# Two rows of weights side by side over the first chunk of x

## The chip, the cores and the metric

The kernel runs on one core of a Trainium2 chip. The metric is the device time in microseconds of one execution; a kernel's time is the median of its runs. The engines are named as in the profile: PE is TensorE (matmuls), PEld its weight loads, DVE is VectorE, ACT is ScalarE, POOL is GpSimd, SP is SyncE, which here only issues DMAs. ACT issues a few DMAs too.

## The reference

One inference step of a two-layer decoder trunk: a prompt of 1024 tokens and 8 x 4 sample tokens, 1056 tokens in all, of width 1024. Layer 0 is a gated linear recurrence with a short convolution, layer 1 a gated linear recurrence with a matrix state; a final norm follows. What matters here is how layer 0 starts:

```
xf = x.astype(jnp.float32)
xn = xf * lax.rsqrt(jnp.mean(xf * xf, axis=-1, keepdims=True) + EPS) * gain
u = xn @ w_in                       # (tokens, 1024) @ (1024, 3072)
xb, gate = u[..., :W_LRU], u[..., W_LRU:]
xc, new_buf = _causal_conv(xb, conv_w, conv_b, buf)
h, h_last = _rg_lru(xc, w_r, b_r, w_i, b_i, lam, h0)
y = h * silu(gate)
x = x + y @ w_out
```

## The kernel before

Everything lies transposed: features on the 128 partitions, tokens along the free dimension. The 1056 tokens are three chunks of 352 (`CH`, index `c`), the 1024 features of x eight blocks of 128 (index `k`). A row of weights is one 128-wide slice of the output features: 128 x 1024 numbers, which come in two halves of 512 columns; the first half serves blocks 0 to 3 of x, the second blocks 4 to 7.

Each fp32 operand is split into a rounded part and a remainder, hi and lo, and a product takes three matmuls (`mm3`, lines 241 to 245: hi by hi, lo by hi, hi by lo). For a half row of weights that means one DMA into `wraw` (or another free tile: `a`, `ST`), one cast on ACT into `whi` (L378) and one subtraction into `wlo` (L323). For a block of x of the first chunk it is one DMA into `sg`, one ACT instruction into `xh` (L861) and one DVE instruction into `xl` (L867). The step of a row over one block is the three matmuls, and eight steps fill one PSUM bank of the four called `mm` (mm_156 to mm_159, taken in turn).

The first chunk is not normalised before it is multiplied. Its squares are summed aside (`squares`: L428 on POOL or L430 on ACT, then the sums on DVE, L433, into `xb`), `norm` (L277, L445 to L453) makes the factor of each token, and the evacuation of a bank multiplies by it (L527 for a gate row, L480 for a convolution row). Chunk 1 is normalised first (L458, its sums of squares in `R`), then split again (L459, L323) and multiplied. Six rows come first, three gate rows and three convolution rows (`items = gate(0) + conv(0, True)`); `products(c)` goes through them chunk by chunk. Row 4 is the fifth, and takes the bank of row 0 again.

48 dummy matmuls (`WARM`, L728: ones by ones into a bank that nobody reads) keep PE busy until the first data are there. They wait for nothing and have the lowest priority.

The order on all five engines comes from a planner. The code of the layer first records operations in a `Flow` (engine, estimated us, what is read, what is written, a priority); `plan` lists them by priority as they become ready, `back` derives due times from the end, eight turns of that are tried, and `search` then changes keys at random in the first 60 us, 3000 times with a fixed seed, and keeps what brings a late PE instruction no later. What is recorded with `main=True` keeps its own order: each main PE operation depends on the one recorded before it, so the steps run in the order in which they are recorded. For these first products each step is an operation of its own (`product(..., 1, ...)`). The order found is written into the program as it stands, so each engine goes through its list in order and waits where something isn't there yet.

```
def product(w, xs, step=8, more=()):
    ps, pk = next(mm)
    ...
        fl.add("PE", 0.48 * len(ks), emit, (...), (pk,), 1, main=True)
    return ps, pk
```

## Time and profile before

| what | us |
|---|---|
| three runs | 1062.17, 1062.39, 1063.31; median 1062.39 |
| the profiled execution | 1062.88 |
| its span, first to last instruction | 1061.1 |
| PE busy in the span | 1051.4 |
| DVE busy | 843.7 |
| ACT busy | 588.2 |
| POOL busy | 542.0 |

The profile shows one execution. A line of instructions gives start and duration in us, engine, source line, operation, written tile and read tiles, shapes, and how many; in brackets the engine's idle time before it and what ended that. Matmuls are pipelined: one of 352 columns is shown with 0.32 us, but the next starts 0.16 us later, so a step takes 0.48. PE being busy therefore does not say that it does useful work: the dummies count too.

### The profile page before, as it was taken

What the parts mean: (1) busy time and instruction counts of PE and PEld (TensorE: products, weight loads), DVE (VectorE), ACT (ScalarE), POOL (GpSimd) and SP (SyncE); (2) the same over time, 40 slices, a digit from 0 to 9 for tenths busy, and PEclk for the clock granted to TensorE, in tenths of its full rate; (3) what the DMA queues carried; (4) which work ended last, traced back from release to release, by engine and by line L of the source; (5) the groups of instructions that cost most, each with busy time, mean ns of one, the idle gap of its engine ahead of it and who ended that gap; (6) DMA issues with size and microseconds to landing.
All of it is one profiled execution on the core that took longest, in us unless ns stands there. A gap on an engine that the chain in (4) does not pass through costs nothing.

```text
span 1061.1 us, 25695 instructions
## 1 busy us (share of the span) xinstructions
PE 1051.4 (99%) x9972; PEld 1025.8 (97%) x9972; DVE 843.7 (80%) x1677; ACT 588.2 (55%) x1329; POOL 542.0 (51%) x604
## 2 busy tenths in 40 slices
PE   9999999999999999999999999999999999999997
PEld 9999999999999999999999999999999999999996
DVE  7999996888888689265799988978879797994435
ACT  6568656867675875243354474646464645652323
POOL 3425443444444455555677656555555565642544
PEclk9999999999999999999999999999999999999997
DMA  9201112123742685440210131312121212354204
GB/s 301 64 26 45 54 51 74 57 61 108 240 150 61 182 287 165 133 130 28 73 51 30 44 101 45 101 37 89 44 83 53 85 58 74 113 181 156 85 1 164
DMA packets 70121, 103.07 MB, mean 97 GB/s; under 512 B 9200, under 2 KB 51184, under 8 KB 70000
## 3 DMA queue, kind: packets, MB, share of 16 engines
q1 hardware_dynamic: 67696, 98.67, 29.9%
q10 hardware_dynamic: 2304, 2.77, 0.8%
q8 instruction: 78, 1.28, 0.5%
q14 instruction: 43, 0.35, 0.1%
HBM read 71.05 MB, written 25.49 MB: 91 GB/s over the span
## 4 chain that ended last, share of the span: by engine, by line
PE 89%; DVE 7%; POOL 1%; DMA 1%; issue 1%; ACT 0%; POOLq 0%; ACTq 0%; DVEq 0%
PE mm L243 24%; PE mm L244 24%; PE mm L245 24%; PE hg L567 1%; PE hg L1052 1%; PE hg L1161 1%; PE hg L1271 1%; DVE R L1368 1%; PE hg L1217 1%; PE hg L243 1%; PE hg L244 1%; PE hg L245 1%; PE hg L1273 1%; DMA wraw<-in_w_dram 1%; DVE tmp L1368 1%
## 5 line engine op out<-in xcount | busy, mean ns | idle before, releaser
L243 PE MATMUL mm<-xh,whi 128*128 128x352 f32 (+1 forms) x1143 | 358.8, 314 | 0.0
L245 PE MATMUL mm<-xh,wlo 128*128 128x352 f32 (+1 forms) x1143 | 353.4, 309 | 0.0
L244 PE MATMUL mm<-xl,whi 128*128 128x352 f32 (+1 forms) x1143 | 353.4, 309 | 0.0
L323 POOL TENSOR_TENSOR wlo<-wraw,whi 128x256 fp32r<-128x256 f32 (+3 forms) x184 | 203.2, 1121 | 178.7 <-ACT whi L378 79.9
L244 PEld LDWEIGHTS mm<-xl,whi 128*128 128x128 f32 x1143 | 215.3, 188 | 1.5
L243 PEld LDWEIGHTS mm<-xh,whi 128*128 128x128 f32 x1143 | 215.0, 188 | 1.5
L245 PEld LDWEIGHTS mm<-xh,wlo 128*128 128x128 f32 x1143 | 215.0, 188 | 0.0
L499 DVE SCALAR_TENSOR_TENSOR k<-xb,prm_sb,k 128x352 f32<-128x352 f32 (+2 forms) x144 | 90.0, 636 | 10.9 <-ACT k L496 7.7
L243 PE MATMUL mm<-t,whi 128*128 128x264 f32 (+1 forms) x306 | 89.4, 292 | 0.0
L244 PE MATMUL mm<-t,whi 128*128 128x264 f32 (+1 forms) x306 | 87.8, 287 | 0.0
L245 PE MATMUL mm<-t,wlo 128*128 128x264 f32 (+1 forms) x306 | 87.6, 286 | 0.0
L1501 DVE TENSOR_TENSOR k<-mm,k 128x264 f32<-128x264 f32 x144 | 60.2, 426 | 20.6 <-PE mm L245 17.5
L323 POOL TENSOR_TENSOR wlo<-R,whi 128x256 fp32r<-128x256 f32 x64 | 60.0, 957 | 24.7 <-ACT whi L1428 24.7
L582 POOL TENSOR_TENSOR k<-X 128x352 f32<-128x352 f32 x36 | 43.9, 1228 | 47.8 <-DVE R L583 38.2
L378 ACT CAST whi<-wraw 128x512 fp32r<-128x512 f32 (+2 forms) x83 | 46.1, 574 | 30.0 <-PE mm L244 15.7
L243 PEld LDWEIGHTS mm<-t,whi 128*128 128x128 f32 x306 | 57.7, 188 | 0.2
L245 PEld LDWEIGHTS mm<-t,wlo 128*128 128x128 f32 x306 | 57.8, 189 | 0.0
L244 PEld LDWEIGHTS mm<-t,whi 128*128 128x128 f32 x306 | 57.7, 189 | 0.0
L1428 ACT CAST whi<-wraw 128x512 fp32r<-128x512 f32 x52 | 32.1, 619 | 36.3 <-PE mm L245 16.8
L243 PE MATMUL mm<-yh,whi 128*128 128x352 f32 x153 | 50.0, 327 | 0.0
L245 PE MATMUL mm<-yh,wlo 128*128 128x352 f32 x153 | 49.4, 323 | 0.0
L244 PE MATMUL mm<-yl,whi 128*128 128x352 f32 x153 | 49.4, 323 | 0.0
(479 smaller groups left out, 2640.9 us busy)
## 6 DMA issues: line engine op xcount, KB each, us to landing
wraw<-in_w_dram SPq DMA_DIRECT2D x90, 256.0 KB, 2.8
wraw<-in_wo_dram SPq DMA_DIRECT2D x34, 192.0 KB, 2.6
si<-in_s_in_dram SPq DMA_DIRECT2D x8, 512.0 KB, 3.6
out_ss_out_dram<-si SPq DMA_DIRECT2D x8, 512.0 KB, 2.6
R<-in_w_dram SPq DMA_DIRECT2D x15, 256.0 KB, 2.6
sg<-x1b SPq DMA_DIRECT2D x21, 176.0 KB, 3.0
x<-sg SPq DMA_DIRECT2D x21, 176.0 KB, 1.9
R<-td SPq DMA_DIRECT2D x72, 44.0 KB, 2.0
```

Of the source, the lines that this page charges most:

```text
L243: T.matmul(out, wh, xh, start=first, stop=False)
L244: T.matmul(out, wh, xl, start=False, stop=False)
L245: T.matmul(out, wl, xh, start=False, stop=last)
L323: emit = lambda: e.tensor_tensor(b, x, a.bitcast(F32), op=ALU.subtract)
L378: act(m, lambda hi=hi, raw=raw, m=m: S.copy(hi[:, :m], raw[:, :m]), rk, (hk,), prio)
L499: dve(u, lambda src=src, dst=dst, sh=sh, k=k: V.scalar_tensor_tensor(dst, sh(src, k), pc("cw", 12 * k + m), dst, op0=ALU.mult, op1=ALU.add ...
L567: fl.add("PE", 0.62, lambda ps=ps, i=i, c=c: T.matmul(ps[:96, :CH], gs[:, i, :], ST[:96, chunk(c)], start=True, stop=True), (("gs",), *((" ...
L582: pool(CH, lambda x=x, a=a, b=b: G.tensor_tensor(x, a.bitcast(F32), b.bitcast(F32), op=ALU.add), (ak, bk), (xk,), 3)
L1052: T.matmul(ps[32 * j:32 * j + 32, n * w:n * w + w], B[:, o:o + 32], q(slice(o, o + 32)), start=True, stop=True, tile_position=(0, 32 * j))
L1368: dve(n, lambda: V.tensor_tensor(o, a, b, op=op), r, (w,), prio, True)
L1428: act(512, lambda: S.copy(hi, raw), (rk,), (hk,), 2)
L1501: dve(QT, lambda: V.tensor_tensor(o[0], z[0], u[0], op=ALU.add), (z[1], u[1]), (o[1],), 0)
```

## The change

`side_by_side` takes the first two rows (`SIDE = 2`, both gate rows) over chunk 0. It takes a bank for each, and records the steps block by block: block 0 for row 0, block 0 for row 1, block 1 for row 0, and so on; then both banks are evacuated. The other four rows, and all rows over chunks 1 and 2, are recorded as before.

```diff
+SIDE = 2
...
+        def side_by_side(w, xs):
+
+            got = [next(mm) for _ in w]
+            n = len(xs)
+            for k in range(n):
+                for i, (ps, pk) in enumerate(got):
+                    fl.add("PE", 0.48, lambda k=k, i=i, ps=ps: mm3(ps[:, :CH], w[i](k)[:2], *xs[k][:2], k == 0, k == n - 1),
+                           (*xs[k][2], *w[i](k)[2]), (pk,), 1, main=True)
+            return got
+
         def products(c):
-            for i in (2, 0, 1, 3, 4, 5) if c else range(6):
+            if c == 0:
+                for i, got in enumerate(side_by_side(ws[:SIDE], xcols(0))):
+                    items[i][1](0, *got, bcs)
+            for i in (2, 0, 1, 3, 4, 5) if c else range(SIDE, 6):
                 items[i][1](c, *product(ws[i], xcols(c), 1, more=later[i]), *([] if c else [bcs]))
```

Since the planner lists the operations anew, more moves than the diff says, on all engines; the order is the same again after some 440 matmuls on PE, 307 instructions on DVE, 217 on ACT, 86 on POOL and 75 on SP. In the new kernel the lines from 32 on stand one line lower (L244 is the L243 of before), so the pieces are shown apart.

PE at its start, before. In the names, mm_156 is row 0's bank and mm_157 row 1's; xh_93, xh_95, xh_97 and xh_99 are blocks 0 to 3; whi_122 is row 0's first half.

```order
L728 MATMUL hg_160<-ones_80 128x128 x29
L243 MATMUL mm_156<-xh_93,whi_122 128x352
L244 MATMUL mm_156<-xl_94,whi_122 128x352
L245 MATMUL mm_156<-xh_93,wlo_126 128x352
L243 MATMUL mm_156<-xh_95,whi_122 128x352
L244 MATMUL mm_156<-xl_96,whi_122 128x352
L245 MATMUL mm_156<-xh_95,wlo_126 128x352
L728 MATMUL hg_160<-ones_80 128x128 x9
L243 MATMUL mm_156<-xh_97,whi_122 128x352
```

PE at its start, now; whi_124 and wlo_128 are row 1's first half.

```order
L729 MATMUL hg_160<-ones_80 128x128 x29
L244 MATMUL mm_156<-xh_93,whi_122 128x352
L245 MATMUL mm_156<-xl_94,whi_122 128x352
L246 MATMUL mm_156<-xh_93,wlo_126 128x352
L729 MATMUL hg_160<-ones_80 128x128 x18
L244 MATMUL mm_157<-xh_93,whi_124 128x352
L245 MATMUL mm_157<-xl_94,whi_124 128x352
L246 MATMUL mm_157<-xh_93,wlo_128 128x352
L244 MATMUL mm_156<-xh_95,whi_122 128x352
```

All but one of the dummies now stand ahead of row 1's first step, 18 of them in one block behind row 0's first; one more follows after block 2. Before, they stood in five gaps between row 0's steps.

DVE and the DMAs that feed it at the start. SP's queue before (`sg` is x, `wraw_121` is row 1's second half, `a_112` its first; both halves of row 0, wraw_119 and wraw_120, are issued by ACT in both kernels):

```order
L310 DMA wraw_121<-in_w0_dram 128x512
L310 DMA sg_147<-in_xT_dram 128x352 x2
L310 DMA a_112<-in_w0_dram 128x512
L310 DMA sg_147<-in_xT_dram 128x352
L310 DMA sg_149<-in_xT_dram 128x352
L310 DMA sg_148<-in_xT_dram 128x352
```

SP's queue now:

```order
L311 DMA sg_147<-in_xT_dram 128x352 x2
L311 DMA sg_145<-in_xT_dram 128x352
L311 DMA wraw_121<-in_w0_dram 128x512
L311 DMA sg_147<-in_xT_dram 128x352
L311 DMA sg_148<-in_xT_dram 128x352
L311 DMA sg_149<-in_xT_dram 128x352
L311 DMA sg_148<-in_xT_dram 128x352
L311 DMA a_112<-in_w0_dram 128x512
```

Three pieces of x go first (two of the first chunk, and sg_145, which holds a piece of chunk 1), and row 1's first half goes from fourth to ninth place. On ACT's queue the gain g0 (4 KB) goes ahead of wraw_119. DVE before, its first instructions that are not small (wlo_126 and wlo_127 are row 0's halves, wlo_129 row 1's second):

```order
L323 TENSOR_TENSOR wlo_129<-wraw_121,whi_125 128x512
L740 TENSOR_SCALAR smalls_84<-smalls_84 128x12
L323 TENSOR_TENSOR wlo_126<-wraw_119,whi_122 128x512
L867 SCALAR_TENSOR_TENSOR xl_94<-sg_147,g0_164,xh_93 128x352
L867 SCALAR_TENSOR_TENSOR xl_96<-sg_147,g0_164,xh_95 128x352
L433 TENSOR_TENSOR xb_0_132<-xb_0_132,xo_0_135 128x352
L323 TENSOR_TENSOR wlo_127<-wraw_120,whi_123 128x512
```

DVE now:

```order
L868 SCALAR_TENSOR_TENSOR xl_94<-sg_147,g0_164,xh_93 128x352
L868 SCALAR_TENSOR_TENSOR xl_96<-sg_147,g0_164,xh_95 128x352
L324 TENSOR_TENSOR wlo_126<-wraw_119,whi_122 128x512
L741 TENSOR_SCALAR smalls_84<-smalls_84 128x12
L324 TENSOR_TENSOR wlo_127<-wraw_120,whi_123 128x512
L324 TENSOR_TENSOR wlo_129<-wraw_121,whi_125 128x512
L434 TENSOR_TENSOR xb_0_132<-xb_0_132,xo_0_135 128x352
```

The two `xl` go to the front, and row 1's second half goes behind row 0's two.

DVE at the split of chunk 1, before; PE needs these `xl` (xl_94 block 0, xl_96 block 1, xl_98 block 2, xl_102 block 4, xl_104 block 5) for the first row of that chunk:

```order
L323 TENSOR_TENSOR xl_94<-sg_144,xh_93 128x352
L323 TENSOR_TENSOR xl_98<-sg_146,xh_97 128x352
L480 TENSOR_TENSOR xb_2_134<-mm_156,R_73 128x352
L458 SCALAR_TENSOR_TENSOR sg_146<-sg_146,g0_164,hg_160 128x352
L323 TENSOR_TENSOR xl_96<-sg_145,xh_95 128x352
L458 SCALAR_TENSOR_TENSOR sg_149<-sg_149,g0_164,hg_160 128x352
L323 TENSOR_TENSOR xl_104<-sg_146,xh_103 128x352
L458 SCALAR_TENSOR_TENSOR R_73<-R_73,g0_164,hg_160 128x352
L323 TENSOR_TENSOR xl_102<-sg_145,xh_101 128x352
```

Now:

```order
L324 TENSOR_TENSOR xl_102<-sg_145,xh_101 128x352
L459 SCALAR_TENSOR_TENSOR sg_146<-sg_146,g0_164,hg_160 128x352
L324 TENSOR_TENSOR xl_96<-sg_145,xh_95 128x352
L459 SCALAR_TENSOR_TENSOR sg_146<-sg_146,g0_164,hg_160 128x352
L324 TENSOR_TENSOR xl_94<-sg_144,xh_93 128x352
L324 TENSOR_TENSOR xl_98<-sg_146,xh_97 128x352
L459 SCALAR_TENSOR_TENSOR sg_149<-sg_149,g0_164,hg_160 128x352
L459 SCALAR_TENSOR_TENSOR R_73<-R_73,g0_164,hg_160 128x352
L324 TENSOR_TENSOR xl_104<-sg_146,xh_103 128x352
```

Block 4 has gone from the end to the front, block 0 from the front to the fifth row, and the evacuation of row 4's bank (L480 into xb_2) has left this stretch; it now stands behind two sums of squares (L434) and one L459.

## The prediction

> **What bounds the kernel now.** I read the page's first lines, then what TensorE waited for, then the stages, then the first 45 us instruction by instruction, because the diff reaches only there.
>
> ```profile
> span 1061.1 us, 25695 instructions
> PE 1051.4 (99%) x9972; PEld 1025.8 (97%) x9972; DVE 843.7 (80%) x1677; ACT 588.2 (55%) x1329; POOL 542.0 (51%) x604
> ```
>
> TensorE (PE) is busy for 99% of the span, so whatever PE idles less or more at the start goes to the end one to one, unless a later wait takes it up. All its waits in the whole run are these (columns: total us, times, longest us):
>
> ```profile
> PE hg L728 <- DVE ones L255: 1.0, 1, 1.0
> PE mm L243 <- DVE sg L527: 0.7, 1, 0.7
> PE hg L1106 <- DVE a L1034: 0.5, 1, 0.5
> PE hg L277 <- ACT sg L1726: 0.4, 1, 0.4
> PE hg L1052 <- DVE R L1064: 0.4, 1, 0.4
> ```
>
> The first is the wait for the first instruction, the last three lie in the second layer, where the two kernels have the same order. One wait is within reach: 0.7 us behind L527 of VectorE (DVE). By stretches (us, then busy us of PE, PEld, DVE, ACT, POOL; clock, DMA share, GB/s):
>
> ```profile
> 0.00:6.48 6.48, 5.45 (x30) 5.45 (x31) 1.63 (x13) 2.76 (x6) 0.97 (x9) 1.00 0.69 206
> 6.48:31.41 24.93, 24.82 (x179) 24.32 (x177) 24.00 (x47) 18.82 (x42) 12.41 (x11) 1.00 0.82 277
> 31.41:42.74 11.33, 10.71 (x63) 10.12 (x63) 11.33 (x24) 7.09 (x15) 4.98 (x6) 1.00 0.29 87
> 42.74:75.00 32.26, 32.21 (x199) 31.76 (x200) 31.40 (x81) 18.71 (x44) 8.50 (x14) 1.00 0.09 24
> ```
>
> From 6.48 to 42.74 us DVE is busy for 35.33 of 36.26 us: while PE looks full, DVE is what is short. The rows of PE tell how both can be full:
>
> ```profile
> 9.62 0.41 PE L243 MATMUL mm<-xh,whi 128*128 128x352 f32 x1
> ...
> 10.66 2.17 PE L728 MATMUL hg<-ones 128*128 128x128 f32 x18
> 12.59 0.41 PE L243 MATMUL mm<-xh,whi 128*128 128x352 f32 x1
> ...
> 14.79 1.27 PE L728 MATMUL hg<-ones 128*128 128x128 f32 x10
> 15.82 0.41 PE L243 MATMUL mm<-xh,whi 128*128 128x352 f32 x1
> ...
> 31.98 0.42 PE L243 MATMUL mm<-xh,yh 128*128 128x352 f32 x1 [0.68 <-DVE sg L527]
> ...
> 42.79 0.43 PE L244 MATMUL mm<-xl,X 128*128 128x352 f32 x1
> ...
> 44.66 0.32 PE L243 MATMUL mm<-xh,whi 128*128 128x352 f32 x1
> ```
>
> The gaps between the first row's steps hold no idling: they hold the dummy matmuls of L728, 18 records there (two records to an instruction, so 9 instructions), then 4, 2, 10 and 4. After them PE stops twice: at 31.98, where row 4 needs the bank that L527 empties, and at 42.79, where the second chunk's `xl` is late.
>
> **The change, part by part.**
>
> *The interleaving itself: 0.* The same 16 steps and the same 48 dummies are issued; the order shows 29, 18 and 1 dummies where there were 29, 9, 2, 1, 5 and 2. A dummy in a gap and a dummy ahead of it cost the same. So the gap total, (12.59 - 10.66) + (15.82 - 14.79) and the shorter ones, some 3.8 us, is not to be had: the dummies have to run somewhere before step 16. Returning from dummies to steps costs a little (a first matmul of 0.41 against 0.32), and there are three such returns fewer, about 0.3 us; but PE then waits at row 4 for DVE anyway, which swallows it. The cover is that wait; without it this would be a gain of 0.3.
>
> So the question is when DVE gets to L527 of bank mm_156 (31.41 before; call it S), and how long after S the first row of chunk 1 ends (44.66 before, so S + 13.25). Up to S the two orders hold the same 61 DVE instructions, but for one L527 that empties another bank. Only the waiting among them can differ.
>
> *First term, S.* These rows set the start of DVE:
>
> ```profile
> 4.56 0.69 DVE L323 TENSOR_TENSOR wlo<-wraw,whi 128x512 fp32r<-128x512 f32 x1
> 6.48 1.11 DVE L323 TENSOR_TENSOR wlo<-wraw,whi 128x512 fp32r<-128x512 f32 x1 [1.15 <-ACT whi L378]
> 7.52 1.07 DVE L867 SCALAR_TENSOR_TENSOR xl<-sg,g,xh 128x352 fp32r<-128x352 f32 x2
> 8.51 0.51 DVE L433 TENSOR_TENSOR xb<-xb,xo 128x352 f32<-128x352 f32 x1
> 9.01 0.69 DVE L323 TENSOR_TENSOR wlo<-wraw,whi 128x512 fp32r<-128x512 f32 x1
> 9.62 1.27 DVE L323 TENSOR_TENSOR wlo<-a,whi 128x512 fp32r<-128x512 f32 x1
> ```
>
> ```profile
> 5.83 0.62 ACT L378 CAST whi<-wraw 128x512 fp32r<-128x512 f32 x1 [1.10 <-DMA wraw<-in_w_dram]
> 8.36 0.62 ACT L378 CAST whi<-wraw 128x512 fp32r<-128x512 f32 x1 [0.43 <-DMA wraw<-in_w_dram]
> ```
>
> ```profile
> sg<-in_xT_dram SPq DMA_DIRECT2D x15, 176.0 KB, 4.6
> wraw<-in_w_dram ACTq DMA_DIRECT2D x2, 256.0 KB, 5.4
> prm_sb<-in_prm_dram ACTq DMA_DIRECT2D x1, 72.0 KB, 3.1
> g<-in_prm_dram ACTq DMA_DIRECT2D x1, 4.0 KB, 4.7
> ```
>
> DVE waits for casts, and the casts wait for transfers. Before, the first eight transfers are 72 + 4 + 4 weights of 256 + 2 of x of 176 = 1452 KB, and the last of them releases the cast at 8.36. In the new order they are 72 + 4 + 3 x 256 + 3 x 176 = 1372 KB: x has been put ahead and one weight half has gone back behind. 80 KB less is worth little, so I let row 0's second half land at the same 8.3. Before that moment the old order gives DVE two `wlo`, two `xl` and one `xb`, and by 9.62 a third `wlo`: 3 x 0.61 + 2 x 0.49 + 0.43 = 3.24 us of work (start to start: 9.62 - 9.01 for a `wlo`, half of 8.51 - 7.52 for an `xl`; an `xb` takes 0.43, being 0.51 less the overlap of 0.08). The new order has only two `xl` and one `wlo` (1.59 us), then stands until the cast ends at 8.36 + 0.62 = 8.98, and does its second `wlo` by 9.6: 2.20 us. DVE is 1.04 us behind. Some of it is made up, because the summing of squares ahead of S is paced by ACT:
>
> ```profile
> 23.96 2.40 DVE L433 TENSOR_TENSOR R<-R,xo 128x352 f32<-128x352 f32 x4
> ```
>
> Four sums take 2.40 us there, 0.60 each, though one alone needs 0.43; a late DVE finds its operands ready for a few of them, at 0.17 us each. I take 0.6 us as what is left of the 1.04. Ends: 1.5 above (nothing made up and one more stall of the kind in which DVE waits for POOL: the `wlo` of 9.62 took 1.27, the others 0.69); -0.5 below (one such stall fewer, as at 6.48 and 9.62). Queued behind the waiting cast on ACT are the other row's cast and the `xh` of the later blocks of x, which stood behind a cast at the same 8.36 before, too; DVE alone waits for them, PE being still at its dummies. The queues that things are moved past: on SP, x moves past weights, priced here; on ACT's queue the 4 KB of `g` move past a weight, which only helps the first `xl`; POOL keeps its instructions up to S in nearly the same order, 0.
>
> *Second term, from S to the end of the row.*
>
> ```profile
> 31.41 0.95 DVE L527 TENSOR_TENSOR sg<-mm,R 128x352 f32<-128x352 f32 x2
> ...
> 32.61 1.32 DVE L451 TENSOR_SCALAR k<-ident,nr 128x96 f32<-128x96 f32 x1
> 33.84 0.51 DVE L480 TENSOR_TENSOR xb<-mm,R 128x352 f32<-128x352 f32 x1
> 34.28 1.92 DVE L529 SCALAR_TENSOR_TENSOR sg<-k,sg 128x352 f32<-128x352 f32 x3
> 36.12 2.53 DVE L458 SCALAR_TENSOR_TENSOR sg<-sg,g,hg 128x352 f32<-128x352 f32 x5
> 38.58 0.94 DVE L323 TENSOR_TENSOR xl<-sg,xh 128x352 fp32r<-128x352 f32 x2
> ...
> 42.23 0.94 DVE L323 TENSOR_TENSOR xl<-sg,xh 128x352 fp32r<-128x352 f32 x2
> ```
>
> Before, `xl_102` (block 4) comes last and is done at 42.74; PE waits for it at block 4, with a gap of 0.26 us and about 0.1 of restart. In the new order `xl_102` comes early and one L480 has gone behind the `xl`; the late one is `xl_94` (block 0). From S to its end: L527 twice and L480 once at 0.43, the two of `k` 0.33 + 0.18, three L529 1.29, one small 0.08, six L458 at 0.49 (2.46 / 5) = 2.94, two `xl` at 0.43 and the last 0.51 = 7.48, and the stalls of before (32.61: 1.32 of which 0.27 is its own; 34.28: three in 1.92 instead of 1.38) 1.05 + 0.54 = 1.6, together S + 9.1. PE, let go at S + 0.57 (31.98 - 31.41), needs what it needed before for rows 4 and 5, 8.46 us, so it is there at S + 9.03: it waits about 0.1, then takes its eight steps of 0.48. The row ends at S + 13.0 instead of 13.25: **-0.25**. Ends: -0.35 (no wait left), +0.6 (one more stall of about 0.9). The two sums of squares and the L480 put behind are covered by the stretch to 75 us, in which PE has no wait; should that cover go, they cost 3 x 0.43.
>
> *Sum:* 0 + 0.6 - 0.25 = +0.35 us. The profiled execution took 1062.88 us for its span of 1061.1; the median of the three runs shown is 1062.39. Against the profile 1063.23, against the median **1062.7**. What a measurement can tell from no change is about 0.2%, 2.1 us; this lies well within.
>
> **Rivals.**
>
> *DVE is not late (S moves by 0 or less).* For it: x comes first, so the first `xl` can start before 6.48, and the stalls with POOL may fall better. Against: the two second halves of weights are again the seventh and eighth transfer. It gives 0 - 0.25 to -0.5 - 0.35, so 1062.1 to 1061.5; I name 1061.9.
>
> [...]
>
> *Slower: the second halves of the weights land late.* Place: DVE between its first `wlo` and its second, with nothing to do; every us of delay is a us of S. With the second term at -0.25, S has to move by 2.4 us before it shows as slower; the cast would have to start at about 10.2 instead of 8.36. For it: weights now share the first microseconds with three pieces of x, and SP's later transfers wait for earlier ones. Against: fewer bytes lie ahead. Time at 2.9: 1065.0.
>
> *The gaps were real.* If the dummies shrank out of the way, PE would win up to 3.8 us: 1058.6. Against it: all 48 stand in the new order.
>
> **How the numbers follow.** Forecast case 0.57, DVE not late 0.27, weights late 0.13, gaps real 0.03. The first two are both within 0.2%: 0.84. The range goes from the lower ends (-0.5 - 0.35, and 0.3 for the spread of the runs) to the upper ends (1.5 + 0.6, and again the spread): 1061.2 to 1064.9.
>
> **What would show it.** Right: PE still without a gap from 1.03 to past 25 us, steps in pairs after a block of 36 records of L728; DVE idle for a microsecond or two before its second `wlo`; L527 of mm_156 at about 32.0; a PE wait at row 4 of about 1.6 us (0.68, the 0.3 that PE saves, and the 0.6) and then 13.0 us to the end of the next chunk's first row; everything from 75 us on shifted by the same few tenths. Wrong: a PE wait before row 2, or a new one between 45 and 75 us, or a shift of L527 beyond 2 us.

## The result and the profile after

The changed kernel takes 1065.62 us (median of 7 runs, 1064.64 to 1066.24), the kernel before 1062.17 us in the same comparison (7 runs, 1061.32 to 1063.31): 1.0033 times as long, 95% interval 1.0024 to 1.0043. That is 3.4 us slower, and the interval does not reach 1. The forecast was 1062.7 us with a range up to 1064.9.

The page's first lines and what PE waited for most, of the changed kernel (lines of the code are one further than before up to the new function, and fourteen further behind it):

```profile
span 1063.8 us, 25686 instructions
PE 1054.1 (99%) x9972; PEld 1028.6 (97%) x9972; DVE 845.3 (79%) x1677; ACT 588.7 (55%) x1329; POOL 541.9 (51%) x604
```

```profile
PE hg L278 <- DVE R L434: 1.4, 1, 1.4
PE hg L729 <- DVE ones L256: 1.0, 1, 1.0
```

The other three are those of the second layer, now 0.4, 0.3 and 0.2 us. The wait of 0.7 us at row 4 is gone. In its place stands one of 1.4 us, at L278: the norm_sum of chunk 1, which waits for a sum of squares on DVE (L434). Yet PE is busy 2.7 us longer than before, 1054.1 us instead of 1051.4, with as many instructions. So waits are not where most of the loss is; something makes the same work slower. By two stretches of the prediction, and then by finer ones:

```profile
6.48:31.41 24.93, 23.57 (x166) 22.74 (x165) 22.68 (x45) 17.43 (x38) 8.47 (x9) 0.96 0.83 284
31.41:42.74 11.33, 11.33 (x66) 11.12 (x65) 11.22 (x23) 7.07 (x16) 5.92 (x6) 0.93 0.29 88
...
26.12:29.53 3.41, 2.05 (x15) 1.71 (x14) 3.26 (x8) 1.72 (x5) 1.64 (x2) 1.00 0.04 11
29.53:32.94 3.41, 3.41 (x12) 2.92 (x11) 3.24 (x10) 2.90 (x7) 1.72 (x2) 0.50 0.40 118
32.94:36.36 3.42, 3.42 (x23) 3.42 (x22) 3.42 (x6) 1.93 (x5) 3.12 (x4) 1.00 0.52 138
```

The granted clock, 1.00 before until the last 11 us of the run, falls here to 0.50 from 29.53 to 32.94 us: 12 records of PE in 3.41 us, and 23 in the 3.42 us behind. PE instruction by instruction:

```profile
10.28 4.18 PE L729 MATMUL hg<-ones 128*128 128x128 f32 x36
...
28.19 0.78 PE L278 MATMUL hg<-ones,R 128*128 128x1 f32 x6 [1.36 <-DVE R L434]
...
31.64 0.50 PE L245 MATMUL mm<-xl,yh 128*128 128x352 f32 x1
31.94 0.49 PE L246 MATMUL mm<-xh,yl 128*128 128x352 f32 x1
...
34.17 0.32 PE L245 MATMUL mm<-xl,yh 128*128 128x352 f32 x1
34.33 0.32 PE L246 MATMUL mm<-xh,yl 128*128 128x352 f32 x1
34.49 0.32 PE L244 MATMUL mm<-xh,yh 128*128 128x352 f32 x1
```

At half clock a matmul starts every 0.30 us (31.64, 31.94), at full clock every 0.16 (34.17, 34.33). Row 4 begins at 34.49; before it began at 31.98. DVE and POOL around that wait, and two rows of DVE in the kernel before:

```profile
7.47 0.69 DVE L324 TENSOR_TENSOR wlo<-wraw,whi 128x512 fp32r<-128x512 f32 x1 [1.40 <-ACT whi L379]
...
8.84 1.87 DVE L324 TENSOR_TENSOR wlo<-wraw,whi 128x512 fp32r<-128x512 f32 x2 [0.60 <-ACT whi L379]
...
21.08 1.15 DVE L434 TENSOR_TENSOR R<-R,xo 128x352 f32<-128x352 f32 x2
...
25.23 2.91 DVE L434 TENSOR_TENSOR R<-R,xo 128x352 f32<-128x352 f32 x3
...
28.66 0.41 DVE L449 TENSOR_TENSOR k<-ident,nr 128x256 f32<-128x256 f32 x1
...
32.20 0.95 DVE L528 TENSOR_TENSOR sg<-mm,R 128x352 f32<-128x352 f32 x2
```

```profile
25.34 1.15 POOL L448 TENSOR_TENSOR nr<-nr,mhalf 128x3 f32<-128x3 f32 x1 [1.27 <-DVE nr L446]
26.46 1.29 POOL L324 TENSOR_TENSOR yl<-wraw,yh 128x512 fp32r<-128x512 f32 x1
```

```profile
26.36 0.42 DVE L448 TENSOR_TENSOR k<-ident,nr 128x256 f32<-128x256 f32 x1
...
26.88 2.69 DVE L433 TENSOR_TENSOR R<-R,xo 128x352 f32<-128x352 f32 x3
```

Three sums take 2.91 us while POOL runs its pow and a subtraction; alone one needs 0.43. The third of them ends at 28.1, and that is what the norm_sum waits for. The second L528 of 32.20, at 32.63, empties the bank of row 0: S, 31.41 before, is 32.63. The kernel before has such a slow stretch too (three sums in 2.69 us from 26.88, beside POOL's subtraction of 1.69 us at 26.86), but behind the norm_sum, which starts at 27.04 there.

That is the first 75 us. The second place of the loss lies where the two orders are the same. Three landmarks of PE, each a single matmul that both kernels have: in the first gate product of the recurrence, in layer 0's last third, and ahead of the last wait of the run. First the kernel before, then the changed one:

```profile
88.12 0.46 PE L567 MATMUL hg<-ST,gs 96*96 96x352 f32 x1
460.44 0.46 PE L453 MATMUL hg<-xb,ones 128*128 128x352 f32 x1
1048.15 0.25 PE L277 MATMUL hg<-ones,sg 128*128 128x1 f32 x1
```

```profile
90.11 0.46 PE L568 MATMUL hg<-ST,gs 96*96 96x352 f32 x1
464.27 0.46 PE L454 MATMUL hg<-xb,ones 128*128 128x352 f32 x1
1052.78 0.25 PE L278 MATMUL hg<-ones,sg 128*128 128x1 f32 x1
```

The shift is 1.99 us at the first landmark, 3.83 at the second and 4.63 at the third. So 2.64 us come up between 88 and 1048 us, most of them before 540 us, with no wait to show for it: in layer 0 the matmuls with 352 columns start 161.0 ns after one another instead of 159.6 (means over some 1780 pairs of neighbouring matmuls on `xh` and `xl` in each trace between 92 and 540 us).

And a part is given back at the end. From the third landmark to the end of the span (stretch, then as above; the kernel before first, the changed one below):

```profile
1048.15:1061.07 12.92, 6.12 (x32) 5.31 (x31) 4.55 (x12) 2.22 (x5) 4.66 (x6) 0.57 0.53 186
```

```profile
1052.78:1063.83 11.05, 4.23 (x32) 3.55 (x31) 4.52 (x12) 2.21 (x5) 4.61 (x6) 0.84 0.63 217
```

The same 32 records run at a mean clock of 0.57 there and of 0.84 here, and 1.87 us of the 4.63 are won back. This end took between 11.05 and 12.92 us in the twenty profiled executions of this study. With one of them for each kernel, no pattern by kernel can be read from it; the spread of the runs of a kernel, some 2 us, is of that size, and in e10 below the run of 1061.66 us has a mean clock of 0.999, the ten from 1063.2 to 1064.77 us one of 0.994 to 0.997. Times of single kernels that are less than a microsecond apart are therefore not told from one another below, and the landmarks, which lie ahead of that end, are read beside the times.

### The profile page after: what moved, and what is told of

Same layout as the page of the kernel before. It is cut to its first block, busy times and chain, and to the rows that moved or that the text cites. A ratio compares the mean times of both kernels' runs of the same rounds, so it can differ in the third digit from the quotient of the medians.

```text
span 1063.8 us, 25686 instructions
## 1 busy us (share of the span) xinstructions
PE 1054.1 (99%) x9972; PEld 1028.6 (97%) x9972; DVE 845.3 (79%) x1677; ACT 588.7 (55%) x1329; POOL 541.9 (51%) x604
## 3 DMA queue, kind: packets, MB, share of 16 engines
q8 instruction: 78, 1.28, 0.5%
## 4 chain that ended last, share of the span: by engine, by line
PE 91%; DVE 6%; POOL 1%; DMA 1%; issue 1%; ACT 0%; ACTq 0%; POOLq 0%; DVEq 0%
PE mm L244 25%; PE mm L245 25%; PE mm L246 25%; PE hg L568 1%; PE hg L1066 1%; PE hg L1175 1%; PE hg L1285 1%; DVE R L1382 1%; PE hg L1231 1%; PE hg L244 1%; DMA wraw<-in_w_dram 1%; PE hg L246 1%; PE hg L245 1%; PE hg L1287 1%; DVE tmp L1382 1%; DVE R L1048 1%
## 5 line engine op out<-in xcount | busy, mean ns | idle before, releaser
L244 PE MATMUL mm<-xh,whi 128*128 128x352 f32 (+1 forms) x1143 | 358.8, 314 | 0.0
L324 POOL TENSOR_TENSOR wlo<-wraw,whi 128x256 fp32r<-128x256 f32 (+3 forms) x184 | 206.0, 1135 | 181.5 <-ACT whi L379 88.2
L244 PEld LDWEIGHTS mm<-xh,whi 128*128 128x128 f32 x1143 | 215.4, 188 | 1.7
L244 PE MATMUL mm<-t,whi 128*128 128x264 f32 (+1 forms) x306 | 89.4, 292 | 0.0
L244 PEld LDWEIGHTS mm<-t,whi 128*128 128x128 f32 x306 | 57.7, 189 | 0.2
L244 PE MATMUL mm<-yh,whi 128*128 128x352 f32 x153 | 50.0, 327 | 0.0
```

Of the source, the lines that this page charges most:

```text
L244: T.matmul(out, wh, xh, start=first, stop=False)
L324: emit = lambda: e.tensor_tensor(b, x, a.bitcast(F32), op=ALU.subtract)
```

## The experiments

Shifts at the three landmarks, in us against the kernel before, are worked out from the same three rows of each trace; the last column is what came up between the first and the third. "Before" in a comparison is the kernel before, run beside it on the same chip.

| kernel | median us | before beside it | ratio (95%) | at 88 | at 460 | at 1048 | from 88 to 1048 |
|---|---|---|---|---|---|---|---|
| changed | 1065.62 | 1062.17 | 1.0033 (1.0024, 1.0043) | 1.99 | 3.83 | 4.63 | 2.64 |
| e3 rows in turn, old plan | 1061.74 | 1061.52 | 0.9999 (0.999, 1.0007) | -0.02 | -0.02 | -0.01 | 0.01 |
| e4 row by row, new plan | 1065.55 | 1061.52 | 1.0033 (1.002, 1.0045) | 1.74 | 3.58 | 4.39 | 2.65 |
| e1 six dummies | 1065.52 | 1061.52 | 1.0035 (1.0022, 1.0049) | 1.61 | 3.46 | 4.31 | 2.70 |
| e2 norm_sum later | 1065.82 | 1061.52 | 1.0032 (1.002, 1.0045) | 0.90 | 2.75 | 3.50 | 2.60 |
| e5 old places | 1064.03 | 1061.74 | 1.0020 (1.0011, 1.0029) | 1.99 | 1.98 | 2.27 | 0.28 |
| e6 before, new places | 1064.39 | 1061.74 | 1.0021 (1.0012, 1.0029) | 0.34 | 2.19 | 3.41 | 3.07 |
| e7 old places of x | 1063.94 | 1061.74 | 1.0019 (1.0011, 1.0028) | 2.04 | 2.03 | 2.23 | 0.19 |
| e8 old places of weights | 1065.93 | 1061.74 | 1.0036 (1.0024, 1.0049) | 1.57 | 3.42 | 4.17 | 2.60 |
| e9 e2 and e7 together | 1063.35 | 1062.20 | 1.0009 (1.0000, 1.0018) | 0.74 | 0.74 | 0.66 | -0.08 |
| e10 two tiles exchanged | 1064.19 | 1062.20 | 1.0019 (1.0011, 1.0028) | 1.66 | 1.69 | 1.98 | 0.32 |
| e11 before, odd pairs | 1065.10 | 1062.20 | 1.0033 (1.0021, 1.0046) | 0.14 | 2.36 | 3.89 | 3.75 |
| e12 before, x 64 bytes on | 1063.20 | 1062.20 | 1.0010 (1.0001, 1.0019) | 0.34 | 1.11 | 1.47 | 1.13 |
| e13 before, runs alike | 1062.72 | 1061.62 | 1.0011 (1.0002, 1.0020) | -0.09 | 0.27 | 0.83 | 0.92 |
| e14 before, runs alike, odd first | 1061.96 | 1061.62 | 1.0000 (0.9991, 1.0009) | 0.61 | 0.80 | 0.94 | 0.33 |
| e15 e2 with runs alike | 1063.98 | 1061.62 | 1.0019 (1.0010, 1.0028) | 1.52 | 1.88 | 2.33 | 0.81 |
| e16 e9, POOL later | 1063.74 | 1062.46 | 1.0014 (1.0005, 1.0023) | 1.30 | 1.30 | 1.62 | 0.32 |
| e17 changed, other draw | 1064.05 | 1062.46 | 1.0017 (1.0008, 1.0025) | 2.13 | 2.12 | 2.41 | 0.28 |
| e18 before, other draw | 1065.45 | 1062.46 | 1.0029 (1.0018, 1.0041) | 4.51 | 4.51 | 4.67 | 0.16 |

The landmarks scatter too. With the orders of the kernel before, the first one lies between -0.09 and 0.61 us (e3, e6, e11 to e14), with those of the changed kernel between 1.57 and 2.04 (changed, e5, e7, e8, e10), with those of e2 between 0.74 and 1.52 (e2, e9, e15). Differences of half a microsecond there, and up to 0.8 within the last group, are not told from chance. The last column is steadier: 2.60 to 2.70 in the five kernels that keep the changed kernel's places of x (changed, e1, e2, e4, e8), -0.08 to 0.32 in the seven with those of before (e3, e5, e7, e9, e16 to e18) and in e10.

In the diffs, `arrange` gets the order that the search found and returns the one that is written out; `seq` is that order split by engine. The numbers are those of the planner's operations: 225 to 240 the sixteen steps as the changed kernel records them, block by block (in the kernel before row 0 is 225 to 232 and row 1 is 236 to 243), 258 to 265 the steps of row 3, 194 the norm_sum of chunk 1, 144 the matmul of chunk 0's factor (L454), 166 the first half of `yl` for row 5 and 197 chunk 1's pow. `moved(seq, i, j)` puts i behind j.

### Is it the rows in turn, or the plan that came with them?

The change gives the planner another list of work, and so another plan on all engines. Two kernels take the two apart: each keeps one plan and only exchanges the sixteen steps on PE among their places.

```diff
 the kernel before
+    steps = iter([i for k in range(8) for i in (225 + k, 236 + k)])
+    seq["PE"] = [next(steps) if 225 <= i <= 232 or 236 <= i <= 243 else i for i in seq["PE"]]
 the changed kernel
+    steps = iter([225 + i for i in (*range(0, 16, 2), *range(1, 16, 2))])
+    seq["PE"] = [next(steps) if 225 <= i <= 240 else i for i in seq["PE"]]
```

> The kernel before, every engine's order as it was, except that the 16 steps of the first two rows stand on TensorE in turn, block by block (the 16 places, the dummies between them and all else stay). Theory B (the loss comes from the plan that the search found for the changed list of work, not from the steps in turn): 1062.2, at most 0.7 away from it, no drop of the clock. Rival C (the steps in turn cost by themselves, through the two banks or through row 0 ending late): 1065.

> The opposite: the changed kernel with every engine's order as the change has it, except that the 16 steps stand on TensorE row by row again. Theory B: the stall at the norm_sum is still there, 1.0 to 1.4 us, and the drop of the clock too: 1065.2 to 1065.8. Rival C: 1062.3.

With the old plan the rows in turn cost nothing: 0.9999, and the three landmarks to 0.02 us:

```profile
88.10 0.46 PE L594 MATMUL hg<-ST,gs 96*96 96x352 f32 x1
460.42 0.46 PE L480 MATMUL hg<-xb,ones 128*128 128x352 f32 x1
1048.14 0.25 PE L304 MATMUL hg<-ones,sg 128*128 128x1 f32 x1
```

PE waits 0.3 us for row 1's first `wlo` there and comes to row 4 later, where it then waits 0.15 us instead of 0.68; so the half microsecond that the turns cost PE is covered by that wait. With the new plan, row by row, all of the loss is there: 1065.55. PE waits 1.24 us at the norm_sum in it, as expected, but the clock doesn't drop, which wasn't. The loss belongs to the plan, its orders and what follows from them, and the steps in turn are innocent.

### The stall at the norm_sum

Two ways to take it off PE: filling it, and moving what stalls.

```diff
 e1, the changed kernel
+    at = order.index(194)
+    return order[:at] + [0] * 6 + order[at:]
 e2, the changed kernel
+    self.moved(seq["PE"], 194, 262)
+    self.moved(seq["PE"], 144, 264)
```

> The changed kernel with six more dummy matmuls (0.21 us each, 1.28 us) right ahead of the norm_sum of chunk 1, where TensorE stood for 1.36 us. The norm_sum can start no earlier than before, at 28.19. Theory A (the stall costs its own length and then 1.7 us more, because the granted clock is 0.5 for 3.41 us behind it): the clock stays at 1.00 through 45 us, row 4 begins 1.3 to 1.7 us earlier than its 34.49, and the time is 1065.6 - 1.5 = 1064.1. Rival (the stall alone counts, or the loss lies elsewhere): 1065.6, with or without the drop of the clock. Rival (the dummies just push the norm_sum back): 1066 or more.

> The changed kernel with chunk 1's norm_sum moved behind block 4 of row 3 and the matmul of L454 behind block 6, on TensorE alone. DVE reads that sum only at 30.9, so nothing waits for it. Theory A: no wait at the norm_sum; TensorE then comes to row 4 at about 31.2 and waits there for the bank that L528 empties at 33.1, 1.9 us. So the stall moves rather than goes. If a wait of 1.9 us there lowers the clock as the 1.36 us did: 1065.2 to 1066.0. If it does not: 1064.2. Rival (the place of the norm_sum is the whole loss): 1062.3.

The clock did stay at 1.00 in both until the end of the run. Of e1, the stretches to be compared with those above:

```profile
26.12:29.53 3.41, 2.92 (x24) 2.73 (x23) 3.26 (x5) 2.02 (x5) 1.95 (x2) 1.00 0.27 100
29.53:32.94 3.41, 3.41 (x22) 3.16 (x21) 3.19 (x12) 2.59 (x6) 1.41 (x2) 1.00 0.42 123
```

But row 4 began 0.97 us earlier (33.52) and the first landmark only 0.38 us (1.61 against 1.99), not 1.5: with PE faster, row 4 waits for the bank again, and S, 32.95 in this execution, sets its start. e1's time of 1065.52 is a miss of the expected 1064.1. In e2 the stall moved to row 4, as expected, with a full clock:

```profile
28.82 0.67 PE L305 MATMUL hg<-ones,R 128*128 128x1 f32 x6
...
32.81 0.43 PE L271 MATMUL mm<-xh,yh 128*128 128x352 f32 x1 [1.16 <-DVE sg L555]
```

There the shift is 0.90 us at 88 us, 1.1 less than in the changed kernel, and 3.50 against 4.63 at 1048. The time doesn't show it (1065.82, where 1064.2 was expected). One profiled execution says 1.1 us for the place of the norm_sum, the other two with this order say 1.25 and 0.5 (e9, e15), and the runs say less than their spread; that is as far as it goes. The drop of the clock is worth less still: e8, of the next part, has the changed kernel's orders, waited 1.12 us at the norm_sum and kept its clock of 1.00, and it is 1.57 us behind at 88 us, where those with a drop are 1.66 to 2.04 behind. What both runs leave standing is the 2.6 us behind 88 us.

### Where the tiles lie

The order of the two kernels is the same behind 75 us, name by name, but names are not places. `new_acts` takes the sixteen tiles of `xh` and `xl` from one ring of sixteen buffers, the weights and the long work rows come from such rings too, and a tile gets its buffer when its first instruction is written out. Another order of first writers gives other places in SBUF. As the built programs have it, in buffers of 4224 bytes from the start of the ring:

```
block          0   1   2   3   4   5   6   7
before   xh    0  15  12   9   8   5  11   4
         xl   14  13  10   7   6   3   1   2
changed  xh    0  15  12  11   7   4   9   3
         xl   14  13  10   8   5   2   6   1
```

Four kernels pin tiles to chosen buffers, each by a ring of its own, with all orders unchanged:

```diff
+    def placed(pool, shape, dt, tag, names, slots):
+        made = {}
+        for n, s in sorted(zip(range(len(slots)), slots), key=lambda q: q[1]):
+            made[n] = pool.tile(shape, dt, tag=f"{tag}{s}", bufs=1, name=names[n])
+        return [made[n] for n in range(len(slots))]
+
     def new_acts():
-        hs, ls = [], []
-        ...
-        return hs, ls
+        both = placed(acts, [128, TOK], F32R, "P", ("xh", "xl") * KD, [0, 14, 15, 13, 12, 10, 9, 7, 8, 6, 5, 3, 11, 1, 4, 2])
+        return both[::2], both[1::2]
```

> The changed kernel with all orders as they are, but with the tiles of x (xh, xl), of the weights (wraw, whi, wlo) and the nine long work rows (a, ST, sg) pinned to the SBUF places that they have in the kernel before. In the changed kernel their first writers come in another order, and the pool gives out places in that order. Theory P (places): of the shift against the kernel before, 2.0 us stand at 75 us and 2.65 us more come up evenly from 90 to 1049 us, in which TensorE runs the very same instructions; with the old places that second part is gone. The starts at 90 and at 1049 us then differ from those of before by the same 2.0, and the time is 1065.5 - 2.6 = 1062.9. Rival (the drift comes from the two more instructions in TensorE's stream, from the semaphores or from the other engines' lag): 1065.5, still 2.6 us of drift.

> The kernel before, every order as it was, with the places of the changed kernel for the same tiles. Theory P: nothing differs up to 45 us, then TensorE loses 2.6 us by 1049 us against before: 1061.7 + 2.6 = 1064.3. Rival: 1061.7.

> The changed kernel with the old places for xh and xl alone. If it is where x lies that sets the rate of the matmuls: 1062.9. If it is where the weights or the work rows lie: 1065.5. If it is how x and the weights lie to one another: between them, or worse than 1065.5.

> The changed kernel with the old places for wraw, whi and wlo alone. If it is where the weights lie: 1062.9. If it is x or the work rows: 1065.5.

The kernel before with the new places, and nothing else changed, is 2.65 us slower (1064.39 against 1061.74), and its landmarks drift as the changed kernel's do:

```profile
88.46 0.46 PE L569 MATMUL hg<-ST,gs 96*96 96x352 f32 x1
462.63 0.46 PE L455 MATMUL hg<-xb,ones 128*128 128x352 f32 x1
1051.56 0.25 PE L283 MATMUL hg<-ones,sg 128*128 128x1 f32 x1
```

The changed kernel with the old places has lost the drift: 1.99, 1.98, 2.27. The old places of x alone do the same (2.04, 2.03, 2.23), those of the weights alone nothing (1.57, 3.42, 4.17). So it is where `xh` and `xl` lie. Both times miss the expected 1062.9 by more than a microsecond. Against the kernel before beside them they are 2.29 and 2.20 us slower, which is what their third landmark says (2.27 and 2.23); the 1062.9 was reckoned from the changed kernel's time, which is 1.2 us better than its own third landmark, since part of the loss is won back at the end of the run. e9 puts the two remedies together:

> Two edits at once: the changed kernel with chunk 1's norm_sum and the matmul of L454 later on TensorE, and with xh and xl at their old places. If the loss of 3.8 us is the sum of three parts, 1.1 us for the place of the norm_sum, 2.65 us for the places of x, and 0.9 us for a DVE that comes later to the bank, then only the last stays: 0.9 us behind before at 90 us and at 1049 us, and 1061.7 + 0.9 = 1062.6. Rival (the parts overlap): 1063.5 or more.

It came to 1063.35, 1.0009 times before, and to 0.74, 0.74 and 0.66 us at the landmarks: the drift is gone, and what is left at the start has the size that was expected for it. As a time it is some 0.7 us over the expected 1062.6, within what the end of the run varies.

### Which relation of the places

A buffer is 16.5 times 256 bytes long, so neighbouring buffers begin at two different remainders modulo 256. Before, the `xh` and `xl` of every block lie an even number of buffers apart; in the changed kernel those of blocks 3 and 6 don't (11 and 8, 9 and 6).

```diff
 e10, the changed kernel: buffers 8 and 9 exchanged
-[0, 14, 15, 13, 12, 10, 11, 8, 7, 5, 4, 2, 9, 6, 3, 1]
+[0, 14, 15, 13, 12, 10, 11, 9, 7, 5, 4, 2, 8, 6, 3, 1]
 e11, the kernel before
+[0, 1, 2, 3, 4, 5, 6, 7, 8, 9, 10, 11, 12, 13, 14, 15]
 e12, the kernel before: 64 bytes ahead of the tiles of x
+    pad = pads.tile([128, 16], F32, name="pad")
+    nc.vector.memset(pad, 0.0)
```

> The changed kernel with the places of two tiles exchanged, xl of block 3 and xh of block 6, nothing else. In the kernel before, the xh and xl of each block lie an even number of tiles (4224 B each) apart, so both begin at the same address modulo 256; in the changed kernel two blocks of eight, 3 and 6, do not, and the exchange mends both. Theory Q (a block whose xh and xl begin differently modulo 256 costs): the 2.65 us between 90 and 1049 us go, 1062.9. Rival (some other relation of the places): 1065.5, or any time between.

> The kernel before with xh and xl laid one behind the other, block by block, so that in all eight blocks xh and xl begin differently modulo 256. Theory Q: at least the 2.65 us of two such blocks, up to four times that: 1064.4 to 1072. Rival: 1061.7, or 1064.4 if only two rates exist.

> The kernel before with 64 bytes of padding ahead of the tiles of x, so that x and all that lies behind it begin at 0 modulo 128 instead of 64, and the weights stay at 64. Here too each block's xh and xl begin alike modulo 256. Theory Q: 1061.7. If the remainder modulo 128 itself matters, for x or between x and the weights: up to 3 us on either side of that.

Exchanging two tiles out of sixteen takes the drift away:

```profile
89.78 0.46 PE L569 MATMUL hg<-ST,gs 96*96 96x352 f32 x1
462.13 0.46 PE L455 MATMUL hg<-xb,ones 128*128 128x352 f32 x1
1050.13 0.25 PE L284 MATMUL hg<-ones,sg 128*128 128x1 f32 x1
```

1.66, 1.69, 1.98. As a time that is 1064.19, not the expected 1062.9, but 1.99 us above the kernel before beside it, as the third landmark has it. Eight unequal pairs cost 3.75 us, more than the two but not four times as much. With all pairs equal and x (and all that lies behind it) moved by 64 bytes against the weights, 1.13 us come up, so the pairs aren't the whole of it. Nor is the cost local to the unequal blocks: in the changed kernel the matmuls of blocks 0 to 2, which lie where they lay, are slower as well, by 2.0, 0.3 and 1.1 ns from one to the next, those of the other blocks by 1.4 to 2.3 (means of the rows between 92 and 540 us). A last guess was that each change of remainder between neighbouring matmuls of a row costs, six before:

```diff
 e13, the kernel before; e14 with each number's last bit turned; e15 the layout of e13 in e2
+[0, 2, 4, 6, 8, 10, 12, 14, 1, 3, 5, 7, 9, 11, 13, 15]
```

> The kernel before with x laid so that blocks 0 to 3 (xh and xl) all begin at one remainder modulo 256 and blocks 4 to 7 at the other: of 24 neighbouring matmuls in a row only 2 read from a place that begins differently, where it was 6. Theory R (each such change of remainder costs; 4 more cost 2.65 us, 10 more 3.74): TensorE gains by 1049 us, up to 2.6 us, and the time is 1059.5 to 1061. Theory Q (only unequal pairs cost): 1061.7 as before. Rival (the relation to the weights counts as much): between 1061 and 1063.

> The same with the two remainders exchanged between the blocks. Theories R and Q: as the run before it, within 0.3 us. If the remainder against the weights matters (all weights begin at one remainder), this one and the one before it differ.

> The changed kernel with the norm_sum and the matmul of L454 later and with the same layout of x as two runs above. Start as in the run with the later norm_sum, 0.7 to 0.9 us behind before at 90 us; from there on by theory R up to 2.6 us won: 1060.2 to 1062.0, so that the rows in turn come level with the kernel before or ahead of it. By theory Q: 1062.6 to 1063.3.

It fell: with two changes instead of six nothing is won, 0.92 and 0.33 us are lost behind 88 us, and 1062.72 and 1061.96 are not under the kernel before. e15 is at 1063.98 above what either theory gave. e13 and e14 differ by 0.59 us in that column, more than the 0.3 that both theories allow; with e12 this points to the place against the weights as a second part, which is not shown. Shown is that the two layouts with unequal pairs are slower in this kernel, by 2.6 us with two and 3.75 with eight, and that an exchange that makes two pairs equal again takes the 2.6 us away. These layouts also have more changes of remainder (ten and sixteen), so which relation costs, and by what way, is open.

### The first 75 us: a plan drawn anew

What is left is S, later in every kernel with the new plan. One run takes POOL's subtraction out of the way of the three sums:

```diff
 e16, e9 and
+    self.moved(seq["POOL"], 166, 197)
```

> The changed kernel with the norm_sum and the matmul of L454 later and with the old places of x, and now POOL's first half of yl of row 5 (1.3 us) behind chunk 1's pow instead of ahead of it. Three sums of squares took 2.9 us beside POOL's pow and that subtraction. Theory (they are held up by POOL): they take about 2.2, DVE reaches the bank of row 0 at 31.5 instead of 32.1, and the start is level with before to 0.3 us: 1061.9. Rival (the operands come late anyway, or the collision moves to the next DVE instructions): DVE at 32.0 to 32.6 still, 1062.6 or more.

```profile
24.99 1.79 DVE L463 TENSOR_TENSOR R<-R,xo 128x352 f32<-128x352 f32 x3
...
31.45 0.96 DVE L557 TENSOR_TENSOR sg<-mm,R 128x352 f32<-128x352 f32 x2 [0.51 <-ACT R L904]
32.32 1.51 DVE L478 TENSOR_TENSOR k<-ident,nr 128x256 f32<-128x256 f32 x1
```

The three sums take 1.79 us instead of e9's 2.93, so POOL's subtraction does hold them up. DVE is then ready for the bank at 30.9 us instead of 31.7 but waits 0.51 us for ACT's copy of the factors, and POOL's work, now later, runs beside `k`, which takes 1.51 us instead of e9's 0.86. The start ends up 1.30 us behind before, no better than e9's 0.74, and 1063.74 is the rival's time: the collision moved.

The other two repeat both kernels with another seed of the search, x at its old places:

```diff
-        rng = Random(1)
+        rng = Random(2)
```

> The changed kernel with the old places of x and another seed of the search. If the lag of 1.2 us and the stall at the norm_sum are the luck of the draw: no wait of TensorE at the norm_sum or half of it, 1061.5 to 1062.5. If the list with the rows in turn leads there by itself: 1063 to 1064.

> The kernel before with the old places of x and the same other seed. If draws differ by a microsecond or two: anywhere from 1061 to 1064. If the old list of work is served well by any draw: 1061.7, within 0.4.

The changed kernel has no wait at the norm_sum then, but waits elsewhere, and the kernel before does worse:

```profile
PE mm L244 <- DVE sg L529: 1.2, 1, 1.2
PE hg L455 <- DVE k L453: 1.1, 1, 1.1
```

```profile
PE mm L243 <- ACT xh L862: 1.3, 1, 1.3
...
PE hg L454 <- DVE k L452: 0.8, 1, 0.8
PE hg L283 <- DVE xb L434: 0.6, 1, 0.6
```

(e17 above, e18 below.) With this draw the changed list of work gives 1064.05 us and the old one 1065.45: the sign is turned. Neither run came out as it was expected of luck alone. For the old list the two draws differ by 4.5 us at the first landmark, more than the microsecond or two expected. For the changed list the wait at the norm_sum is gone, yet the shift is 2.13 us, much as before with x at its old places (e7: 2.04), and the time is that expected for a list that leads there by itself, 1063 to 1064. Two draws of each don't settle which. What they do show is that the sign of the difference hangs on the draw, so it says little of what the rows in turn are worth; e3 says that. None of the versions beats the kernel before; e3, which has the rows in turn, equals it.

## Why the prediction was wrong

**The interleaving costs 0: right, by the cover that was named.** e3 shows it with the old plan: PE comes to row 4 half a microsecond later there, not 0.3 earlier, and the wait for DVE swallows it. The 18 dummies (36 records) stand behind the first step, and PE has no gap from 1.03 to 26.84 us.

**"Everything from 75 us on shifted by the same few tenths": this step failed, and cost most.** It took the same order of the same instructions for the same time. The places of x had changed, and 2.64 us came up between the landmarks at 88 and 1048 us (e6: 1064.39 from the places alone). No term of the sum and no rival covered it; the time lies 0.7 us above the range.

**First term, S: the lag was right, its making up was not.** Forecast +0.6, with ends at -0.5 and +1.5; measured +1.22 (32.63 against 31.41). S lies between 31.36 and 32.12 in the seven executions with the old order on DVE and between 32.13 and 33.08 in the ten with the new one, 1.1 us apart in the mean. DVE did stand without work ahead of its first two `wlo` (1.40 and 0.60 us). At 10.64 it had done one `wlo` and one sum less, 0.61 + 0.43 us, than the kernel before at 10.80, so it was 0.88 us behind, where 1.04 was forecast. Of this 0.4 was to be made up, and nothing was: at the first `R` sum (21.08 against 20.61, with one subtraction less and one small instruction more done) it is still 0.9. Then the sums that POOL holds up come ahead of the norm's factor, and `k`, with the same instructions done before it, starts 2.30 us late (28.66 against 26.36). The kernel before has its slow sums behind that point (2.69 us from 26.88), which brings the lag down to 1.22 at S. "POOL keeps its instructions up to S in nearly the same order, 0" was the line that let this pass: the order was nearly the same, but what DVE has to do beside each of them was not.

**What no term had: the norm_sum.** The new plan puts it one block earlier on PE while its sum comes 1.8 us later (28.1 instead of about 26.3, by the rows of L433 and L434): a stall of 1.36 us, with a stretch at half clock behind it in this execution. "A new wait between 45 and 75 us" was named as what would prove the sum wrong; the wait came at 26.84. What it costs is less than its length, since row 4 would have waited for S: row 4 begins 2.51 us late (34.49 against 31.98), of which S explains 1.22; and in e1 and e8, where the clock stays up, S alone sets its start.

**The wait at row 4:** forecast 1.6 us; none in the changed kernel, where the stall ahead used it up, 1.16 in e2, where the stall is gone.

**Second term, -0.25: not there.** In e2 and e1, without a drop of the clock, the shift at 45 us is that of S, 0.9 and 1.6 us: in e1 PE stops short for an `xl` twice (0.13 us at 42.29, 0.05 at 45.82, each with a first matmul of 0.43) where before it stopped once (0.26 us at 42.79), so nothing is gained.

**Rivals.** *Weights late* gave 1065.0, near the result by coincidence, since its mechanism didn't happen: the cast that was to start at 10.2 started at 8.19, before at 8.36. Its row in the changed kernel, behind that of the first half, which did come a microsecond later than before (5.83):

```profile
6.82 0.62 ACT L379 CAST whi<-wraw 128x512 fp32r<-128x512 f32 x1 [1.38 <-DMA wraw<-in_w_dram]
...
8.19 1.14 ACT L379 CAST whi<-wraw 128x512 fp32r<-128x512 f32 x2 [0.45 <-DMA wraw<-in_w_dram]
```

*DVE is not late:* false, S came 1.22 us late. The weights on ACT's queue did not come earlier either: from 2 to 7 us SP's queue moved 604 packets and ACT's 562 before, 564 and 535 now. ACT's queue has the same 576 packets in both kernels, 128 of them for the 4 KB of `g` alone, and its weights are in at 7.7 us in both; the cast of row 0's second half starts at 8.19 us, 0.17 us earlier than before. *The gaps were real:* false, all 48 dummies run.

**The chances.** 0.84 for no measurable change left too little for a plan that is drawn anew. For the old list of work the two seeds give plans 4.5 us apart at the first landmark, and a spread of that kind should have been in the range.

## What to carry to other kernels

An equal list of instructions is not an equal program: where a pool gives out buffers in the order of first use, a change of order at the start moves tiles for the whole run (2.64 us between the landmarks here), so compare addresses too, or pin them. Where a search sets the order, a change of its input is also a new draw: hold the plan fixed and move only the change (as e3 does), or compare several draws of both. And a stall on TensorE should be priced with the clock behind it and against the wait that it replaces, not by its length: here 3.41 us at half clock followed one of 1.36 us, and none followed one of 1.24 us (e4).

## What the runs showed of the hardware

- Where the moving operands lie in SBUF changed the rate of matmuls with 352 columns by 0.9%: 161.0 ns from one to the next in the changed kernel, 159.6 in e7, where only the places of x differ. Two of sixteen tiles decide it (e10, 159.6). The layouts in which some `xh` and `xl` of a block do not begin alike modulo 256 bytes are the slow ones (e6, e11), but that is not all of it (e12), and it is not shown that it is this relation that costs.
- A stall of 1.36 us was followed by half clock. The clock records of the changed kernel have full speed from 5.64 us, half speed from 29.53 us, 23.89 us later (seven times 3.413), for 3.413 us, and full speed again from 32.95. In the 3.41 us ahead of the drop (26.12 to 29.53) PE was busy for 2.05 us, 0.78 us of that with the norm_sum's matmuls of one column.
- Neither the length of the stall nor PE's busy time in the 3.41 us decides it alone. In e15 PE was busy for just 1.70 of the 3.41 us from 31.85 us (row 4's wait of 2.08 us) and the clock stayed at 1.00; in e10 3.41 us with 1.85 us busy, the norm_sum and its wait of 1.56 us in them, were followed by half clock:

```profile
31.85:35.26 3.41, 1.70 (x10) 1.70 (x11) 3.31 (x6) 2.88 (x8) 3.41 (x3) 1.00 0.30 68
```

```profile
25.32:28.73 3.41, 1.85 (x14) 1.56 (x13) 3.20 (x5) 2.19 (x6) 2.21 (x2) 1.00 0.34 120
28.73:32.14 3.41, 3.41 (x11) 2.91 (x11) 3.19 (x13) 2.43 (x7) 1.15 (x2) 0.50 0.39 118
```

  What does go with the drop, in all twenty traces, is PE's busy time less that of the matmuls of one column, read in stretches of 3.41 us along the clock records. Ahead of the end of the run five stretches were followed by half clock, and they are the five with the least of it: 1.00 us (e7), 1.09 (e10), 1.25 (e5), 1.28 (changed) and 1.41 (e18). The next ones, 1.52 (e8, with 2.29 in all) and 1.71 (e15), were not. That the drop comes of this is not shown; no run changes it alone.
